# One core of Trainium2, a two-layer decoder trunk: the first mixer's transposes behind the gate's blocks, both halves' outputs together, the small inverses by one transfer

## The chip, the core and the metric

The kernel runs on one core of one Trainium2 chip. The metric is the device time of an execution in microseconds; the kernel before has a median of 2877.74 us over three runs (2874.36 to 2878.88). Engine names: PE is TensorE's matmul side and PEld its weight load, DVE is VectorE, ACT is ScalarE, POOL is GpSimd, SP is SyncE, which issues most of the DMAs.

## The reference, cut to what matters

Two layers of 2048 columns on 256 rows. Layer 0 is a gated DeltaNet, layer 1 a sparse attention; each is followed by a layer norm, a gated feed-forward block and a gated addition. Only layer 0's mixer is touched:

```python
def gdn_mixer(x, w_in, conv_w, a_log, dt_bias, norm_g, w_o):
    proj = x @ w_in                                   # q, k, v, z, a, b
    qkv = silu(causal_dwconv(qkv, conv_w))            # 4 taps
    ...                                               # 32 value heads, 16 key heads, width 128
    o = gated_delta_rule(q, k, v, g, beta)            # per head: a unit lower triangular solve
    o = o * rsqrt(mean(square(o), -1) + RMS_EPS) * norm_g * silu(z)
    return o.reshape(B, L, GDN_V_W) @ w_o
```

## The kernel before, in words

All products are of float32 values split into a rounded part `hi` (ACT, line 109) and the rest `lo` (DVE, line 110). Weights come in tiles of 128x1024 through the function `weights`: one DMA into `raw` on SP, `hi`, `lo`, three buffers each. `gemm_t_steps` makes products with the weights stationary (`mm_ps`: 8 matmuls of 512 columns with `hi`, line 128, then 8 of 256 columns with `lo`, line 132, per tile); `gemm_steps` makes them with the activations stationary (`b_ps`: per tile 8 matmuls with `hi`, lines 154 and 155, and 4 with `lo`, line 158). Twelve such `b_ps` matmuls are called a block here.

The mixer works on eight groups of four value heads (`gdn_groups`). The tokens stand in two halves a = 0, 1 of 128. Group g goes through these functions:

- `keys`: the projections of k and q, each followed by the convolution (`conv`: on DVE `pd`, three `ac`, on ACT a tanh, on DVE the last product).
- `decays`, `sums`, `blocks` (together `front`): decay factors, norms, and the triangular matrix `L` of each half and head. Its 32x32 diagonal blocks go to DRAM and back into `ld`.
- `substitute`: inverts the diagonal blocks, 62 small operations on POOL (groups 1 to 6) or on DVE (groups 0 and 7). Then four DMAs on POOL's queue write the result `xi` to `tt` in DRAM, and POOL multiplies both halves of `L` by a mask (line 521), which leaves what is below the diagonal blocks.
- `values`: the projection of v with its convolution, and eight transposes `v_ps` (line 547), four for each half, followed by copies on ACT.
- `zgate`: the projection of the gate z, eight blocks of `b_ps`.
- `inverses`: four DMAs on POOL's queue read `tt` into `pm`; `w_ps` = `L` times `pm`, copied into `W` by one ACT operation for each half (line 537).
- `solve`: for each half `pm` times the right side, then three steps `y <- y0 - W y` (`s_ps`, line 526; DVE, line 576); the last one is `u`.
- `outputs`: for each half the product `o_ps` (lines 587, 588), four squares with sums on ACT (`sqs`, line 591), on DVE the mean (`of`, line 592) and an inverse root of 12 operations, four products `ot` (line 598), four transposes `ot_ps` (line 602), and the copies into `oT`.

For one group in program order: `values` of g, `zgate` of g, `keys` of g + 1, `inverses` of g, `front` of g + 1, `substitute` of g + 1, `solve` of g, `outputs` of g. In the last group `ahead` stands in the place of `keys`: it starts the mixer's output projection `x @ w_o` on those rows of `oT` that are there, three steps of two column blocks. A scheduler turns the program into an order for each engine: it takes instructions as they become ready by its own costs, weights first (a priority in `weights`). `after` adds a dependency by hand, without a semaphore unless `sync` is set. PSUM has four banks for `mm_ps` and `b_ps`, two for the tag `bk` (`w_ps`, `s_ps`, `o_ps`, `ot_ps`) and two for the tag `sp`.

Of the kernel before, what the change touches and what calls it, by code (L numbers as in the profile page):

```python
# [27 lines left out]
W_AHEAD = 1000  # L28


C_IDENT, C_TRI, C_OFF, C_CMIN, C_CAUSAL, C_XINIT, C_ONES, C_QMIN = 0, 128, 256, 384, 512, 640, 896, 1024
N_CONST = 1152


def constants():

    c = np.zeros((P, N_CONST), np.float32)
    i, j = np.arange(P)[:, None], np.arange(P)[None, :]
    c[:, C_IDENT:C_IDENT + P] = i == j
    c[:, C_TRI:C_TRI + P] = i <= j  # L40
    c[:, C_OFF:C_OFF + P] = i // 32 > j // 32
# [12 lines left out]
    b = np.where(d < 16, d, np.minimum(large, 31))  # L54
    return c, (np.arange(32)[:, None] == b[None, :]).astype(np.float32)
# [9 lines left out]
class Trunk:  # L65
    def __init__(self, nc, tc, ctx, t):
        self.nc, self.tc, self.t = nc, tc, t
        pool = lambda **k: ctx.enter_context(tc.tile_pool(**k))

        self.const = pool(name="const", bufs=1)  # L70
        self.hl = pool(name="hl", bufs=3)
        self.xtp = pool(name="xtp", bufs=1)
        self.big = pool(name="big", bufs=1)
        self.cp = pool(name="cp", bufs=1, side="right")
        self.wp = pool(name="wp", bufs=3, side="right")
        self.mm = pool(name="mm", bufs=4, space=PSUM)
# [6 lines left out]
        self.offm = cst[:, C_OFF - P:C_OFF - P + P]  # L83
# [297 lines left out]
    def gdn_groups(self, pool, gk, cw, ng, oT, load, gates, ahead):  # L381
# [13 lines left out]
        h4 = range(4)  # L395
        five = lambda ap: ap.rearrange("p (j r) t -> p j r t", r=2)

        def conv(n0, out):

            def done(n, ps):  # L400
                pd = pads[n % 2]
                self.fold(pool, pd[:, 3:], ps)
                ac = pool.tile([P, S], F32, tag="ac", name="ac", bufs=2)
                w = cw[:, :, n0 + n]
                nc.scalar.activation(ac, pd[:, 3:], AF.Identity, scale=w[:, 3:4])
                for k in (2, 1, 0):
                    nc.vector.scalar_tensor_tensor(ac, pd[:, k:k + S], w[:, k:k + 1], ac, op0=ALU.mult, op1=ALU.add)  # L407
                o = out(n)
                nc.scalar.activation(o, ac, AF.Tanh, scale=0.5)
                self.mark = nc.vector.scalar_tensor_tensor(o, o, 1.0, ac, op0=ALU.add, op1=ALU.mult)  # L410
            return done

        def decays(s):
# [88 lines left out]
        def substitute(s, behind=None):  # L502


            L, ld = s["L"], s["ld"]
            eng = nc.gpsimd if behind is None else nc.vector
            xi = pool.tile([P, 8, 32], F32, tag="xi", name="xi", bufs=2)
            tmp = pool.tile([P, 8, 32], F32, tag="xt", name="xt", bufs=2)
# [6 lines left out]
                    self.after(ins, behind)  # L515
                eng.tensor_tensor(xi[:, :m, i + 1:], xi[:, :m, i + 1:], tmp[:, :m, :w], op=ALU.subtract)
            tt = s["tt"] = self.dr.tile([8, 4, 8, 4, 32], F32, tag="tt", name="tt")
            for e in range(4):
                nc.gpsimd.dma_start(out=tt[:, :, :, e].rearrange("q b c j -> (q b) c j"), in_=xi[32 * e:32 * e + 32])
            for a in range(2):  # L520
                nc.gpsimd.tensor_tensor(L[:, a], L[:, a], bcast(self.offm, 4, 1), op=ALU.mult)

        def mul(lhs, rhs, ps=None, first=True, last=True):
            ps = ps if ps is not None else self.sp.tile([P, 4, P], F32, tag="bk", name="s_ps")
            for h in h4:
                nc.tensor.matmul(ps[:, h], lhs[:, h], rhs[:, h], start=first, stop=last)  # L526
            return ps

        def inverses(s):

            for b in range(4):
                nc.gpsimd.dma_start(out=pm[32 * b:32 * b + 32, :, 32 * b:32 * b + 32],
                                    in_=s["tt"][:, b].rearrange("q c e j -> (c e) q j"))
            for a in range(2):
                ps = self.sp.tile([P, 4, 96], F32, tag="bk", name="w_ps")
                mul(s["L"][:, a], pm[:, 4 * a:4 * a + 4, 32:], ps)
                nc.scalar.activation(W[:, a, :, 32:], ps, AF.Copy)

        def values(s):
            g, sv = s["g"], s["sv"]  # L540
            v = pool.tile([P, 4, S], F32, tag="v", name="v")
            self.gemm_t(w_in, 4096 + 512 * g, 512, self.xT, conv(32 + 4 * g, lambda n: v[:, n]))
            vt = s["vt"] = pool.tile([P, 2, 4, P], F32, tag="vt", name="vt")
            for a in range(2):
# [6 lines left out]
        def zgate(s):  # L551
            zs = s["zs"] = pool.tile([P, 2, 512], F32, tag="zs", name="zs")

            def done(a, ps):
                nc.scalar.activation(zs[:, a], ps, AF.Tanh, scale=0.5)
                nc.vector.scalar_tensor_tensor(zs[:, a], zs[:, a], 1.0, ps, op0=ALU.add, op1=ALU.mult)  # L556

            self.gemm(w_in, 8192 + 512 * s["g"], 512, lambda k: self.xT[:, k], KT, done)

        def solve(s):  # L560
            vt = s["vt"]
            u = s["u"] = pool.tile([P, 2, 4, P], F32, tag="u", name="u")
            for a in range(2):
                rhs = vt[:, a]
                if a:
                    ps = mul(s["n21"], u[:, 0])
                    for h in h4:
                        nc.vector.scalar_tensor_tensor(rhs[:, h], ps[:, h], s["nc1"][:, h:h + 1], rhs[:, h],
                                                       op0=ALU.mult, op1=ALU.add)
                y0 = pool.tile([P, 4, P], F32, tag="y0", name="y0")  # L570
                nc.scalar.activation(y0, mul(pm[:, 4 * a:4 * a + 4], rhs), AF.Copy)
                y = y0
                for i in range(3):
                    ps = mul(W[:, a], y)
# [3 lines left out]
        def outputs(s):  # L578

            g, u = s["g"], s["u"]  # L580
            ss = pool.tile([P, 2, 2, 2], F32, tag="oss", name="oss", bufs=2)
            f = pool.tile([P, 2, 2, 2], F32, tag="of", name="of", bufs=2)
            for a in range(2):
                ps = self.sp.tile([P, 4, P], F32, tag="bk", name="o_ps")
                for h in h4:
# [9 lines left out]
                fa = self.rsqrt(pool, f[:, a].rearrange("p j r -> p (j r)"), 4)  # L595
                ot = pool.tile([P, 4, P], F32, tag="y", name="ot", bufs=2)
                for h in h4:
                    nc.vector.scalar_tensor_tensor(ot[:, h], ps[:, h], fa[:, h:h + 1], s["zs"][:, a, h * P:(h + 1) * P],
                                                   op0=ALU.mult, op1=ALU.mult)
                ps = self.sp.tile([P, 4, P], F32, tag="bk", name="ot_ps")  # L600
                for h in h4:
                    nc.tensor.transpose(ps[:, h], ot[:, h], self.ident)
                hi = oT[:, 4 * g:4 * g + 4, 0, a * P:(a + 1) * P]
                lo = oT[:, 4 * g:4 * g + 4, 1, a * P:(a + 1) * P]
                nc.scalar.activation(hi, ps, AF.Identity, scale=ng)
                nc.vector.scalar_tensor_tensor(lo, ps, ng, hi.bitcast(F32), op0=ALU.mult, op1=ALU.subtract)

        def front(s):
            decays(s)
            sums(s)  # L610
            blocks(s)

        n = keys(0)
        front(n)
        for g in range(8):
            s = n
            values(s)
            if not g:
                substitute(s, self.mark)
            zgate(s)  # L620
            if g < 7:
                n = keys(g + 1)
            else:
# [4 lines left out]
            if g < 6:  # L628
                substitute(n)
            solve(s)  # L630
            outputs(s)
            if g == 6:
                substitute(n, s["f"])


    BLOCKS = ((0, 512), (512, 512), (1024, 512), (1536, 512))
# [249 lines left out]
    def run(self, out):  # L886
# [1 line left out]
        begun = [self.project_steps(t["gdn_w_o"], lambda k: self.oT[:, k], 32, i) for i in range(2)]  # L888

        def ahead():  # L890
            for _ in range(3):
                for g in begun:
                    next(g)

# [51 lines left out]
```

## Time and profile before

| | |
|---|---|
| median of three runs | 2877.74 us (2874.36 to 2878.88) |
| the profiled execution | 2870.2 us, its span 2868.4 us |
| PE busy | 2816.9 us, 98% of the span |
| DVE, ACT, POOL busy | 1883.4 us (66%), 1401.6 us (49%), 311.8 us (11%) |
| mean granted clock | 0.995 |

The first mixer takes about the first 790 us of the span; its groups follow each other every 88 us or so. The span is the time from the first to the last instruction of the profiled execution; 1.8 us lie around it. Busy times of PE come from modelled ends of pipelined matmuls, so the profile shows a wait shorter than it is. A wait is written as "who waited <- who released it: us in total, times, longest".

### The profile page before, as it was taken

To read this page: it belongs to the slowest core of one execution; us is meant where nothing else is said; L and a number is where in the kernel's file an instruction comes from. 1 tells how busy PE (TensorE), PEld (TensorE's weight loads), DVE (VectorE), ACT (ScalarE), POOL (GpSimd) and SP (SyncE) were. 2 spreads that over 40 slices of the span, in tenths; PEclk is the share of its full clock that TensorE was granted. 3 is DMA by queue.
4 is the path that set the end of the run, shared out by engine and by line. 5 is a ranking of instruction groups with operands and counts; after the bars stand their busy time and mean duration, and the time that the engine had idled before them with its cause. 6 is when DMAs were issued, how large, how long until landed. Compare 5 with 4: busy or idle time off the path is not lost.

```text
span 2868.4 us, 40302 instructions
## 1 busy us (share of the span) xinstructions
PE 2816.9 (98%) x15022; PEld 2406.3 (84%) x15022; DVE 1883.4 (66%) x3256; ACT 1401.6 (49%) x2147; POOL 311.8 (11%) x580
## 2 busy tenths in 40 slices
PE   8999999999999999999999999999999999999999
PEld 6788888888787888888888888888888888888887
DVE  6878877778655666666554755766576666654565
ACT  4455555555334655555433544455365555543354
POOL 0143234540000000000000000210000000000000
PEclk9999999999999999999999999999999999999999
DMA  6655556655465566666656566554656666656555
GB/s 195 174 154 152 162 158 164 173 151 144 140 221 176 185 201 202 200 204 205 194 194 192 191 190 182 173 157 138 195 167 196 194 191 197 198 191 191 191 190 191
DMA packets 409620, 520.90 MB, mean 182 GB/s; under 512 B 28268, under 2 KB 296944, under 8 KB 409168
## 3 DMA queue, kind: packets, MB, share of 16 engines
q1 hardware_dynamic: 402192, 499.91, 57.4%
q0 software_dynamic: 7232, 18.42, 2.6%
q8 instruction: 118, 1.93, 0.3%
q14 instruction: 78, 0.64, 0.1%
HBM read 514.00 MB, written 7.39 MB: 182 GB/s over the span
## 4 chain that ended last, share of the span: by engine, by line
PE 90%; DVE 5%; ACT 2%; DMA 2%; issue 1%; POOL 0%; SPq 0%; ACTq 0%; DVEq 0%; POOLq 0%
PE mm_ps L128 32%; PE mm_ps L132 16%; PE b_ps L158 12%; PE b_ps L155 11%; PE b_ps L154 11%; PE s_ps L526 2%; DVE lo L110 1%; ACT sqs L591 1%; PE w_ps L526 1%; ACT hi L109 1%; DMA raw<-in_gdn_w_in 1%; PE n_ps L283 1%; DVE ac L407 1%; PE o_ps L588 0%; PE g_ps L479 0%
## 5 line engine op out<-in xcount | busy, mean ns | idle before, releaser
L110 DVE TENSOR_TENSOR lo<-raw,hi 128x1024 fp32r<-128x1024 f32 x925 | 1135.4, 1228 | 805.1 <-ACT hi L109 771.9
L109 ACT ACTIVATE hi<-raw 128x1024 fp32r<-128x1024 f32 x925 | 977.5, 1057 | 1227.7 <-PE b_ps L155 499.9
L128 PE MATMUL mm_ps<-xT,hi 128*128 128x512 f32 x4176 | 1068.1, 396 | 1.1 <-DVE xT L193 1.1
L128 PEld LDWEIGHTS mm_ps<-xT,hi 128*128 128x128 f32 x4176 | 752.8, 190 | 135.7 <-DVE xT L193 1.7
L132 PEld LDWEIGHTS mm_ps<-xT,lo 128*128 128x128 f32 x4176 | 575.3, 190 | 40.9
L132 PE MATMUL mm_ps<-xT,lo 128*128 128x256 f32 x4176 | 602.8, 284 | 0.0
L154 PE MATMUL b_ps<-hi,xT 128*128 128x512 f32 (+1 forms) x704 | 272.3, 389 | 0.4 <-DVE xT L292 0.4
L155 PE MATMUL b_ps<-hi,xT 128*128 128x512 f32 (+1 forms) x704 | 272.5, 389 | 0.0
L154 PE MATMUL b_ps<-hi,hTA 128*128 128x512 f32 x512 | 199.4, 390 | 0.0
L155 PE MATMUL b_ps<-hi,hTA 128*128 128x512 f32 x512 | 199.2, 389 | 0.0
L158 PE MATMUL b_ps<-lo,xT 128*128 128x512 f32 (+1 forms) x704 | 197.1, 392 | 0.0
L155 PEld LDWEIGHTS b_ps<-hi,xT 128*128 128x128 f32 x704 | 133.6, 190 | 25.4 <-issue 0.4
L154 PEld LDWEIGHTS b_ps<-hi,xT 128*128 128x128 f32 x704 | 132.8, 189 | 26.1 <-DVE xT L292 0.7
L158 PEld LDWEIGHTS b_ps<-lo,xT 128*128 128x128 f32 x704 | 130.2, 190 | 25.1
L158 PE MATMUL b_ps<-lo,hTA 128*128 128x512 f32 x512 | 136.9, 389 | 0.0
L205 POOL DMA_DIRECT2D lng<-in_ln_g x16 | 8.7, 546 | 1123.8 <-DVE lo L110 556.4
L158 PEld LDWEIGHTS b_ps<-lo,hTA 128*128 128x128 f32 x512 | 96.1, 188 | 20.0
L155 PEld LDWEIGHTS b_ps<-hi,hTA 128*128 128x128 f32 x512 | 96.1, 188 | 19.9
L154 PEld LDWEIGHTS b_ps<-hi,hTA 128*128 128x128 f32 x512 | 96.1, 188 | 19.9
L154 PE MATMUL b_ps<-hi,oT 128*128 128x512 f32 x256 | 100.4, 392 | 0.3 <-DVE zs L556 0.3
L155 PE MATMUL b_ps<-hi,oT 128*128 128x512 f32 x256 | 100.2, 391 | 0.0
L512 POOL TENSOR_TENSOR xt<-ld,xi 128x60 f32<-128x60 f32 (+24 forms) x186 | 86.0, 462 | 69.3 <-DMA ld<-lt 55.2
(261 smaller groups left out, 2585.7 us busy)
## 6 DMA issues: line engine op xcount, KB each, us to landing
raw<-in_gdn_w_in SPq DMA_DIRECT2D x193, 512.0 KB, 3.9
raw<-in_ffn_w_gate SPq DMA_DIRECT2D x160, 512.0 KB, 3.9
raw<-in_ffn_w_up SPq DMA_DIRECT2D x160, 512.0 KB, 3.6
raw<-in_ffn_w_down SPq DMA_DIRECT2D x160, 512.0 KB, 3.7
raw<-in_dsa_w_in SPq DMA_DIRECT2D x80, 512.0 KB, 3.6
raw<-in_gdn_w_o SPq DMA_DIRECT2D x64, 512.0 KB, 3.7
raw<-in_ple_w_gate SPq DMA_DIRECT2D x64, 512.0 KB, 4.1
raw<-in_dsa_w_o SPq DMA_DIRECT2D x32, 512.0 KB, 3.8
```

The costliest lines, as they stand in the source:

```text
L109: nc.scalar.activation(hi, raw, AF.Copy)
L110: ins = nc.vector.tensor_tensor(lo, raw, hi.bitcast(F32), op=ALU.subtract)
L128: nc.tensor.matmul(q[:m, :], hi[:, k, o:o + m], x[:, k0 + k].rearrange("p a b -> p (a b)"), start=k0 + k == 0, stop=False)
L132: nc.tensor.matmul(q[:m, S:], lo[:, k, o:o + m], x[:, k0 + k, 0, :], start=False, stop=k0 + k == kt - 1)
L154: nc.tensor.matmul(ps[a][:, :n], xh, hi[:, k, :], start=k0 + k == 0, stop=False)
L155: nc.tensor.matmul(ps[a][:, :n], xl, hi[:, k, :], start=False, stop=False)
L158: self.last = nc.tensor.matmul(ps[a][:, :n], x(k0 + k)[:, 0, a * P:(a + 1) * P], lo[:, k, :], start=False, stop=k0 + k == kt - 1)
L283: ins = nc.tensor.transpose(ps[:, k, a * P:(a + 1) * P], x[:, a, (k0 + k) * P:(k0 + k + 1) * P], self.ident)
L407: nc.vector.scalar_tensor_tensor(ac, pd[:, k:k + S], w[:, k:k + 1], ac, op0=ALU.mult, op1=ALU.add)
L512: ins = eng.tensor_tensor(tmp[:, :m, :w], bcast(ld[:, i + 1:, i], m, 1), xi[:, :m, i:i + 1].to_broadcast([P, m, w]), op=ALU.mult)
L526: nc.tensor.matmul(ps[:, h], lhs[:, h], rhs[:, h], start=first, stop=last)
L591: nc.scalar.activation(sq, ps[:, h], AF.Square, accum_out=ss[:, a, h // 2, h % 2:h % 2 + 1])
```

## The change

- `values` no longer issues its transposes; it hands back two functions, one for each half, and `zgate` calls one of the waiting functions after its 4th, 5th, 6th, ... block. Each makes four transposes.
- `outputs` computes `o_ps` and the squares of both halves first, then one inverse root for all eight heads, then the eight products `ot`. Its transposes are handed to the next group's `zgate` in the same way, ahead of that group's `v_ps`; the last group's are issued at the end. A dependency makes the first of four wait for the last of the products.
- In `solve` the second half's product with `pm` waits until all four heads of its right side are there.
- `substitute` writes `xi` by one DMA in the place of four. The mask is gone from the constants and from POOL: `L` stays as it is, and `inverses` copies only the blocks below the diagonal into `W`, by three ACT operations for each half on 32, 64 and 96 partitions.
- Group 0's substitution may start behind the second of the four heads' convolution in the place of the last (`marks[-3]`).
- `ahead` makes five steps of each of its two column blocks in the place of three.

```diff
-            for e in range(4):
-                nc.gpsimd.dma_start(out=tt[:, :, :, e].rearrange("q b c j -> (q b) c j"), in_=xi[32 * e:32 * e + 32])
-            for a in range(2):
-                nc.gpsimd.tensor_tensor(L[:, a], L[:, a], bcast(self.offm, 4, 1), op=ALU.mult)
+            nc.gpsimd.dma_start(out=tt.rearrange("q b c e j -> e (q b) c j"), in_=xi)
...
-                nc.scalar.activation(W[:, a, :, 32:], ps, AF.Copy)
+                for b in (1, 2, 3):
+                    nc.scalar.activation(W[:32 * b, a, :, 32 * b:32 * b + 32], ps[:32 * b, :, 32 * b - 32:32 * b], AF.Copy)
...
-            self.gemm(w_in, 8192 + 512 * s["g"], 512, lambda k: self.xT[:, k], KT, done)
+            for j, _ in enumerate(self.gemm_steps(w_in, 8192 + 512 * s["g"], 512, lambda k: self.xT[:, k], KT, done)):
+                if j > 2 and rest:
+                    rest.pop(0)()
...
-                nc.scalar.activation(y0, mul(pm[:, 4 * a:4 * a + 4], rhs), AF.Copy)
+                nc.scalar.activation(y0, mul(pm[:, 4 * a:4 * a + 4], rhs, start=ins if a else None), AF.Copy)
...
+            fa = self.rsqrt(pool, f.rearrange("p a j r -> p (a j r)"), 8)
+
+            def gate(a):
                 ot = pool.tile([P, 4, P], F32, tag="y", name="ot", bufs=2)
                 for h in h4:
-                    nc.vector.scalar_tensor_tensor(ot[:, h], ps[:, h], fa[:, h:h + 1], s["zs"][:, a, h * P:(h + 1) * P],
-                                                   op0=ALU.mult, op1=ALU.mult)
+                    ins = nc.vector.scalar_tensor_tensor(ot[:, h], parts[a][:, h], fa[:, 4 * a + h:4 * a + h + 1],
+                                                         s["zs"][:, a, h * P:(h + 1) * P], op0=ALU.mult, op1=ALU.mult)
+
+                def turn():
...
+                        t = nc.tensor.transpose(ps[:, h], ot[:, h], self.ident)
+                        if not h:
+                            self.after(t, ins, sync=True)
...
-            values(s)
+            rest += values(s)
             if not g:
-                substitute(s, self.mark)
-            zgate(s)
+                substitute(s, self.marks[-3])
+            zgate(s, rest)
...
-            outputs(s)
+            rest = outputs(s)
...
-            for _ in range(3):
+            for _ in range(5):
                 for g in begun:
                     next(g)
```

The order of the work on PE at the end of group 4's solve, before (`s_ps` is the last product of the solve, `o_ps<-u,qd` the output of the first half, `v_ps` two heads of the next group's values, four transposes):

```order
L128 MATMUL mm_ps<-xT,hi 128x512
L526 MATMUL s_ps<-y,W 128x128 x4
L588 MATMUL o_ps<-u,qd 128x128 x4
L128 MATMUL mm_ps<-xT,hi 128x512 x7
L132 MATMUL mm_ps<-xT,lo 128x256 x8
L547 MATMUL v_ps<-ident,v 128x128 x4
```

and of the change at the same place (`o_ps<-u,qo` opens each head of the second half):

```order
L126 MATMUL mm_ps<-xT,hi 128x512 x2
L522 MATMUL s_ps<-y,W 128x128 x4
L595 MATMUL o_ps<-u,qd 128x128 x4
L594 MATMUL o_ps<-u,qo 128x128
L595 MATMUL o_ps<-u,qd 128x128
```

The second half's output, which stood in the gate's second block, now follows the first half's at once, and the transposes of `v` are gone from ahead of the gate's first block.

The gate's blocks of the next group on PE, before, in the second block:

```order
L602 MATMUL ot_ps<-ident,ot 128x128
L155 MATMUL b_ps<-hi,xT 128x512
L154 MATMUL b_ps<-hi,xT 128x512
L155 MATMUL b_ps<-hi,xT 128x512
L158 MATMUL b_ps<-lo,xT 128x512 x3
L602 MATMUL ot_ps<-ident,ot 128x128
L158 MATMUL b_ps<-lo,xT 128x512
L602 MATMUL ot_ps<-ident,ot 128x128 x2
L587 MATMUL o_ps<-u,qo 128x128
```

and of the change, behind the fourth block:

```order
L153 MATMUL b_ps<-hi,xT 128x512
L156 MATMUL b_ps<-lo,xT 128x512 x4
L614 MATMUL ot_ps<-ident,ot 128x128 x4
L152 MATMUL b_ps<-hi,xT 128x512
L153 MATMUL b_ps<-hi,xT 128x512
```

Four transposes of `ot` stand behind the 4th and behind the 5th block; `v_ps` stand in the same way behind the 6th and the 7th.

PE in group 0, before, from the first sums (`ss_ps`) to the first `w_ps`:

```order
L455 MATMUL ss_ps<-cst,sq 128x1 x4
L479 MATMUL g_ps<-k 128x256 x2
L128 MATMUL mm_ps<-xT,hi 128x512 x2
L132 MATMUL mm_ps<-xT,lo 128x256 x8
L128 MATMUL mm_ps<-xT,hi 128x512 x8
L132 MATMUL mm_ps<-xT,lo 128x256 x8
L128 MATMUL mm_ps<-xT,hi 128x512 x5
L526 MATMUL w_ps<-pm,L 128x96 x8
```

and of the change:

```order
L126 MATMUL mm_ps<-xT,hi 128x512 x6
L453 MATMUL ss_ps<-cst,sq 128x1 x4
L477 MATMUL g_ps<-k 128x256 x2
L522 MATMUL w_ps<-pm,L 128x96 x8
L522 MATMUL s_ps<-vt,pm 128x128 x4
```

In group 0 `w_ps` moves ahead of 15 matmuls with `hi` and 16 with `lo`. In group 7 it stands behind ten blocks of the output projection, where it stood behind six and a half.

## Rows read from the trace of the kernel before

**Rows 1.** The page, busy time by engine.

```profile
PE 2816.9 (98%) x15022; PEld 2406.3 (84%) x15022; DVE 1883.4 (66%) x3256; ACT 1401.6 (49%) x2147; POOL 311.8 (11%) x580
```

**Rows 2.** Windows: one group's stretch; PE, PEld, DVE, ACT, POOL busy, PEclk, DMA, GB/s.

```profile
512.00:600.00 88.00, 87.04 (x515) 75.56 (x515) 69.18 (x160) 47.55 (x92) 37.50 (x74) 1.00 0.59 162
```

**Rows 3.** Waits of PE from 80 to 790 us: us in total, times, longest.

```profile
PE ot_ps L602 <- DVE ot L598: 8.0, 14, 2.0
PE w_ps L526 <- DMA pm<-tt: 6.2, 2, 3.9
PE v_ps L547 <- DVE v L410: 4.6, 9, 1.3
```

**Rows 4.** Timeline of PE, 515 to 542 us: start, us, line, operation, [idle before <- releaser].

```profile
517.83 1.06 PE L588 MATMUL o_ps<-u,qd 128*128 128x128 f32 x8
...
520.34 1.11 PE L132 MATMUL mm_ps<-xT,lo 128*128 128x256 f32 x8
521.30 0.60 PE L547 MATMUL v_ps<-ident,v 128*128 128x128 f32 x4
...
521.97 0.39 PE L155 MATMUL b_ps<-hi,xT 128*128 128x512 f32 x1
...
523.58 1.07 PE L158 MATMUL b_ps<-lo,xT 128*128 128x512 f32 x4
524.49 0.39 PE L154 MATMUL b_ps<-hi,xT 128*128 128x512 f32 x1
...
533.11 0.44 PE L547 MATMUL v_ps<-ident,v 128*128 128x128 f32 x2 [0.31 <-DVE v L410]
...
537.11 0.27 PE L602 MATMUL ot_ps<-ident,ot 128*128 128x128 f32 x1
...
537.45 0.27 PE L602 MATMUL ot_ps<-ident,ot 128*128 128x128 f32 x1
```

**Rows 5.** Timeline of DVE, 515 to 530 us.

```profile
518.15 0.68 DVE L576 TENSOR_TENSOR u<-y,s_ps 128x512 f32<-128x512 f32 x1
...
520.68 0.16 DVE L592 SCALAR_TENSOR_TENSOR of<-oss,wq 128x4 f32<-128x4 f32 x1 [0.23 <-ACT sqs L591]
...
521.99 1.26 DVE L110 TENSOR_TENSOR lo<-raw,hi 128x1024 fp32r<-128x1024 f32 x1
...
525.74 0.34 DVE L598 SCALAR_TENSOR_TENSOR ot<-o_ps,rs,zs 128x128 f32<-128x128 f32 x1
```

**Rows 6.** Groups of instructions on ACT, 80 to 790 us: busy, mean ns, idle before.

```profile
L591 ACT ACTIVATE sqs<-o_ps 128x128 f32<-128x128 f32 x64 | 17.7, 276 | 25.3 <-PE o_ps L588 23.9
...
L537 ACT ACTIVATE W<-w_ps 128x384 f32<-128x384 f32 x16 | 7.8, 491 | 12.3 <-PE w_ps L526 12.3
```

**Rows 7.** Waits of PE from 700 to 800 us (group 7).

```profile
PE w_ps L526 <- DMA pm<-tt: 3.9, 1, 3.9
PE ot_ps L602 <- DVE ot L598: 2.8, 3, 2.0
```

**Rows 8.** Waits of PE from 80 to 160 us (group 0).

```profile
PE v_ps L547 <- DVE v L410: 2.4, 2, 1.3
PE w_ps L526 <- DMA pm<-tt: 2.2, 1, 2.2
PE ss_ps L455 <- ACT sq L452: 0.4, 1, 0.4
```

**Rows 9.** Windows: the stretch behind group 7's wait; PEclk third from the right.

```profile
748.40:751.80 3.40, 3.40 (x19) 3.40 (x18) 0.00 (x0) 0.98 (x2) 0.00 (x0) 0.51 0.02 6
```

**Rows 10.** Chain that ended last, 700 to 800 us (group 7): start, us, what.

```profile
747.98 3.30 PE w_ps L526 x16
```

**Rows 11.** Chain that ended last, 80 to 160 us (group 0).

```profile
126.69 1.71 POOL tt L519 x3
128.40 3.48 DMA tt<-xi
...
138.21 2.00 PE w_ps L526 x16
```

More of the change, by code (lines that the diff above doesn't have):

```diff
@@ L28 @@
 W_AHEAD = 1000
-C_IDENT, C_TRI, C_OFF, C_CMIN, C_CAUSAL, C_XINIT, C_ONES, C_QMIN = 0, 128, 256, 384, 512, 640, 896, 1024
-N_CONST = 1152
+C_IDENT, C_TRI, C_QMIN, C_CMIN, C_CAUSAL, C_XINIT, C_ONES = 0, 128, 256, 384, 512, 640, 896
+N_CONST = 1024
 def constants():
@@ L82, in __init__ @@
         self.tri = cst[:, C_TRI - P:C_TRI - P + P]
-        self.offm = cst[:, C_OFF - P:C_OFF - P + P]
         self.cmin = cst[:, C_CMIN - P:C_CMIN - P + P]
@@ L394, in gdn_groups @@
             nc.gpsimd.memset(pd[:, 0:3], 0.0)
-        h4 = range(4)
+        h4, self.marks = range(4), []
         five = lambda ap: ap.rearrange("p (j r) t -> p j r t", r=2)
@@ L409, in done @@
                 nc.scalar.activation(o, ac, AF.Tanh, scale=0.5)
-                self.mark = nc.vector.scalar_tensor_tensor(o, o, 1.0, ac, op0=ALU.add, op1=ALU.mult)
+                self.marks.append(nc.vector.scalar_tensor_tensor(o, o, 1.0, ac, op0=ALU.add, op1=ALU.mult))
             return done
@@ L502, in substitute @@
         def substitute(s, behind=None):
-            L, ld = s["L"], s["ld"]
+            ld = s["ld"]
             eng = nc.gpsimd if behind is None else nc.vector
@@ L517, in substitute, with mul @@
             tt = s["tt"] = self.dr.tile([8, 4, 8, 4, 32], F32, tag="tt", name="tt")
-            for e in range(4):
-                nc.gpsimd.dma_start(out=tt[:, :, :, e].rearrange("q b c j -> (q b) c j"), in_=xi[32 * e:32 * e + 32])
-            for a in range(2):
-                nc.gpsimd.tensor_tensor(L[:, a], L[:, a], bcast(self.offm, 4, 1), op=ALU.mult)
-        def mul(lhs, rhs, ps=None, first=True, last=True):
+            nc.gpsimd.dma_start(out=tt.rearrange("q b c e j -> e (q b) c j"), in_=xi)
+        def mul(lhs, rhs, ps=None, start=None):
             ps = ps if ps is not None else self.sp.tile([P, 4, P], F32, tag="bk", name="s_ps")
             for h in h4:
-                nc.tensor.matmul(ps[:, h], lhs[:, h], rhs[:, h], start=first, stop=last)
+                ins = nc.tensor.matmul(ps[:, h], lhs[:, h], rhs[:, h], start=True, stop=True)
+                if start is not None and not h:
+                    self.after(ins, start, sync=True)
             return ps
@@ L543, in values, with turn @@
             vt = s["vt"] = pool.tile([P, 2, 4, P], F32, tag="vt", name="vt")
-            for a in range(2):
+            def turn(a):
                 ps = self.sp.tile([P, 4, P], F32, tag="sp", name="v_ps")
@@ L549, in values, with zgate @@
                     nc.scalar.activation(vt[:, a, h], ps[:, h], AF.Identity, scale=sv[:, a, h // 2, h % 2:h % 2 + 1])
-        def zgate(s):
+            return [lambda: turn(0), lambda: turn(1)]
+        def zgate(s, rest):
             zs = s["zs"] = pool.tile([P, 2, 512], F32, tag="zs", name="zs")
@@ L567, in solve @@
                     for h in h4:
-                        nc.vector.scalar_tensor_tensor(rhs[:, h], ps[:, h], s["nc1"][:, h:h + 1], rhs[:, h],
-                                                       op0=ALU.mult, op1=ALU.add)
+                        ins = nc.vector.scalar_tensor_tensor(rhs[:, h], ps[:, h], s["nc1"][:, h:h + 1], rhs[:, h],
+                                                             op0=ALU.mult, op1=ALU.add)
                 y0 = pool.tile([P, 4, P], F32, tag="y0", name="y0")
-                nc.scalar.activation(y0, mul(pm[:, 4 * a:4 * a + 4], rhs), AF.Copy)
+                nc.scalar.activation(y0, mul(pm[:, 4 * a:4 * a + 4], rhs, start=ins if a else None), AF.Copy)
                 y = y0
@@ L582, in outputs @@
             f = pool.tile([P, 2, 2, 2], F32, tag="of", name="of", bufs=2)
+            parts = []
             for a in range(2):
@@ L594, in outputs @@
                 s.setdefault("f", ins)
-                fa = self.rsqrt(pool, f[:, a].rearrange("p j r -> p (j r)"), 4)
+                parts.append(ps)
+            fa = self.rsqrt(pool, f.rearrange("p a j r -> p (a j r)"), 8)
+            def gate(a):
                 ot = pool.tile([P, 4, P], F32, tag="y", name="ot", bufs=2)
                 for h in h4:
-                    nc.vector.scalar_tensor_tensor(ot[:, h], ps[:, h], fa[:, h:h + 1], s["zs"][:, a, h * P:(h + 1) * P],
-                                                   op0=ALU.mult, op1=ALU.mult)
[L600 to L606, printed above, removed]
+                    ins = nc.vector.scalar_tensor_tensor(ot[:, h], parts[a][:, h], fa[:, 4 * a + h:4 * a + h + 1],
+                                                         s["zs"][:, a, h * P:(h + 1) * P], op0=ALU.mult, op1=ALU.mult)
+                def turn():
+                    ps = self.sp.tile([P, 4, P], F32, tag="bk", name="ot_ps")
+                    for h in h4:
+                        t = nc.tensor.transpose(ps[:, h], ot[:, h], self.ident)
+                        if not h:
+                            self.after(t, ins, sync=True)
+                    hi = oT[:, 4 * g:4 * g + 4, 0, a * P:(a + 1) * P]
+                    lo = oT[:, 4 * g:4 * g + 4, 1, a * P:(a + 1) * P]
+                    nc.scalar.activation(hi, ps, AF.Identity, scale=ng)
+                    nc.vector.scalar_tensor_tensor(lo, ps, ng, hi.bitcast(F32), op0=ALU.mult, op1=ALU.subtract)
+                return turn
+            return [gate(a) for a in range(2)]
         def front(s):
@@ L611, in front @@
             blocks(s)
-        n = keys(0)
+        n, rest = keys(0), []
         front(n)
@@ L630, in gdn_groups @@
             solve(s)
-            outputs(s)
+            rest = outputs(s)
             if g == 6:
                 substitute(n, s["f"])
+        for turn in rest:
+            turn()
     BLOCKS = ((0, 512), (512, 512), (1024, 512), (1536, 512))
```

1 line of the change is left out of this document (removed).

## The prediction

> **What bounds the kernel now.** I read the page's busy times first: PE is busy for 2816.9 of 2868.4 us [rows 1]. So a change that gives PE neither more nor less work can gain at most the 51 us in which PE stands still, plus what the profile hides of each wait. Next the windows, to see where PE stands still: a middle group has 87.04 us of PE in 88.00 [rows 2], so most of what is there to gain lies in small pieces. Then the waits of PE over the mixer [rows 3]: the reader is to see three kinds, transposes of outputs that wait for their products (8.0 us, 14 times), transposes of values that wait for the convolution (4.6 us, 9 times), and two waits of `w_ps` for the DMA into `pm` (6.2 us). The change aims at these three and at no other.
>
> These numbers are too small, and the timeline of PE says by how much [rows 4]. Four `b_ps` matmuls start from 523.58 to 524.49 us, 0.227 us apart, but one of them is shown for 0.39 us. So each wait behind such a matmul hides 0.16 us more. 14 x 0.16 = 2.2 and 9 x 0.16 = 1.4 us: the waits are 10.3 us for `ot_ps`, 6.1 us for `v_ps`, 6.5 us for `w_ps`.
>
> **Four in a row.** Is it worth something in itself? From 521.30 to 521.97 us lie four transposes and one `b_ps` matmul [rows 4]: 0.67 - 0.23 = 0.44, 0.11 us for a transpose. From 537.11 to 537.45 us lie one transpose and one `b_ps` matmul between two transposes: 0.34 - 0.23 = 0.11 us. A single one costs no more than one of four, so grouping is worth nothing, and only the waits count. The same holds for the second half's products with `pm`.
>
> **Transposes of outputs.** They move from the second and fourth block to behind the fourth and fifth. PE gets there 4 x 12 x 0.227 = 10.9 us after the gate began, and to the second four 0.44 + 2.7 us later. When are they ready? Now the first product `ot` starts at 525.74 us [rows 5], 4.4 us after the end of the values' projection (521.30 us). The change delays it: DVE's `of` waits for four more squares, 276 ns each [rows 6]; with the reading of the sum I allow 0.5 us each, 2.0 us. So the first product starts 6.4 us after the gate's start. On DVE one `lo` (1.26 us) stands ahead of the fourth product and a second one ahead of the eighth; with 0.34 us for a product [rows 5] four are there after 6.4 + 4 x 0.34 + 1.26 = 9.0 us, eight after 11.6 us. PE needs four at 10.9 and eight at 14.1 us. So these waits go, but for group 7: there no gate follows, 32 `b_ps` matmuls (7.3 us) stand between output and transposes, and the work is longer than before by the four squares and a second `lo`. I leave its waits of 0.8 + 2 x 0.16 = 1.1 us as they are (the 2.8 us of [rows 7] less the 2.0 of group 6). Gain 10.3 - 1.1 = **9.2 us**.
>
> **Transposes of values.** They come behind the sixth and seventh block, 10.9 + 2 x (0.44 + 2.72) = 17.2 us after the gate's start. The last `v` of a group is now waited for in the third block, at 533.11 us [rows 4], 11.8 us after the gate's start. The change puts four more products and the wait for the squares ahead of it: 11.8 + 4 x 0.34 + 2.0 = 15.2 us. So they go in groups 1 to 7: 6.1 less group 0's 2.4 + 2 x 0.16 = 2.7 [rows 8], a gain of **3.4 us**.
>
> **The last inverse.** Group 7's `w_ps` waits 3.9 + 0.16 = 4.1 us for `pm` [rows 7]. Behind it the granted clock is 0.51, that is 1.2 GHz in the place of 2.4 GHz [rows 9]: the 16 matmuls take 3.30 us [rows 10], against 2.00 us in group 0 [rows 11]; with the products behind them I put the loss at 1.6 us. The change lets 120 in the place of 79 `b_ps` matmuls stand ahead, 41 x 0.227 = 9.3 us, and takes three of the four transfers' issue off the chain, 1.7 us [rows 11]. 9.3 is over twice 4.1, so wait and slow clock both go: **5.7 us**.
>
> **Group 0.** Its waits are 2.7 us for `v_ps` and 2.2 + 0.16 = 2.4 us for `w_ps` [rows 8], 5.1 in all. I don't count on them. The order puts `w_ps` ahead of 15 matmuls with `hi` and 16 with `lo`: 15 x 0.227 + 16 x 0.12 = 5.3 us (eight with `lo` take 520.34 to 521.30 us [rows 4]), while the transfer brings `pm` 1.7 us earlier, and what the substitution's earlier start brings no row shows. What was waited for at the transposes is waited for at the sums of squares (`ss_ps`, which already waits 0.4 us) and at `w_ps`. The gain lies between 0 and 5.1; I take **0.5 us**, nearer to the lower end since DVE, the engine waited for, has no less to do there.
>
> **What it costs.** The second half's `o_ps` follows the solve without cover: `u` runs from 518.15 to 518.83 us while the first half's `o_ps` runs from 517.83 us for 8 x 0.11 = 0.9 us [rows 4, 5]; PE can go on with the first pair of the second half for 0.2 us. That just covers it; I charge 0.1 us in seven groups, rounded to **0.5 us** lost. The copies into `W` become three for each half: the row is 491 ns for 384 columns and 276 ns for 128 [rows 6], so 0.83 us in the place of 0.49, hidden behind the product with `pm` (0.9 us) and other matmuls. The mask on POOL and three issues of a DMA in each group leave the path to `pm`, which in groups 1 to 6 nobody waits for: nothing. DVE saves 12 small operations in each group, which shows in no wait of PE: nothing. The one bigger transfer instead of four small ones carries the same bytes in the same pieces: nothing beyond the 1.7 us counted.
>
> **The sum.** 9.2 + 3.4 + 5.7 + 0.5 - 0.5 = 18.3 us. The profiled execution took 2870.2 us, so it would take 2851.9 us. It stands 7.5 us below the median of the runs, 2877.74 us; from the median I forecast **2859 us**. A measurement of this kernel tells about 0.2%, 5.8 us, from no change.
>
> **A rule against it.** After 3.9 us without work PE went to half its clock; after the 2.2 us in group 0 it did not [rows 7, 8, 9]. The Trainium skill, TensorE: Matmul & The Clock Gate, Part 1, says that the array's clock is gated by how busy the engine has been, and that idleness sends it back to half. By that rule a longer wait at group 0's early `w_ps` would cost as much as in group 7, and the sum would be 16.7 us in the place of 18.3.
>
> **The rivals.** *The waits come back in part.* PE, freed of one wait, arrives earlier at the next thing that DVE makes. For it: group 0 looks just so. Against it: in a middle group only 1 us of 88 is idle [rows 2], and DVE is idle for 19 of them. If half of the 12.6 us for `ot_ps` and `v_ps` comes back, the gain is 12 us: 2866 us.
>
> *Group 0's waits go too*, because DVE's earlier start brings `pm` in time: 4.6 us more, 2854 us.
>
> *The transposes wait in full at their new places*, so that the change does not do what it says: 18.3 - 12.6 = 5.7 us, only the last inverse: 2872 us. Against it stand the margins of 1.9 to 2.5 us above.
>
> *Slower: DVE's queue is blocked.* DVE now waits for eight squares at `of`, and the `lo` of the gate's second block stands behind it, now at 521.99 to 523.25 us [rows 5]. PE wants it 8 x 0.227 us into the block that starts at 524.49 us [rows 4], at 526.3 us: 3 us of slack. The price is what the wait exceeds 3 us by, in eight groups. To eat up 18.3 us and 5.8 more, it has to be 6 us, against 2.0 us for four squares: 2884 us or more. The Trainium skill, TensorE: Matmul & The Clock Gate, Architectural detail, says that ACT and DVE take their queues strictly in order, so nothing behind `of` could pass it; the trace agrees, since DVE stood idle for 0.23 us ahead of that `of`, with the `lo` behind it [rows 5].
>
> **How the numbers follow.** The forecast 0.60, waits back in part 0.17, group 0 too 0.10, the transposes wait in full 0.08, slower 0.05. Range 2850 to 2870 us: it takes in the forecast, group 0's gain and the half that comes back, and at the lower end a run that is like the profiled one. Faster by over 0.2%: 0.60 + 0.17 + 0.10 = 0.87; within: 0.08; slower: 0.05.
>
> **What would show it.** Right: no wait `ot_ps <- DVE ot` but about 1 us in group 7; no `v_ps <- DVE v` from group 1 on; no `w_ps` wait and no half clock near 750 us; PE's busy time unchanged within 2 us. In group 0 a wait of 2 to 4 us at `w_ps` near 130 us. Wrong: new waits of `b_ps` for `lo`, or of `o_ps` for `u` by more than 0.3 us each; or the wait of `w_ps` in group 0 gone.

## The result, and the profile after

The changed kernel takes 2896.8 us (median of 6 runs, 2881.8 to 2900.4) beside 2873.5 us for the kernel before (median of 6 as well): a ratio of 1.0075, interval 1.0057 to 1.0093. It is slower by about 0.75%, where the forecast was 2859 us, a gain. The profiled execution took 2900.35 us at a mean granted clock of 0.986 (before: 2870.2 us, 0.995).

Busy times of the changed kernel, from its page; they answer to [rows 1]:

```profile
span 2898.5 us, 40122 instructions
...
PE 2830.6 (98%) x15022; PEld 2425.1 (84%) x15022; DVE 1872.5 (65%) x3160; ACT 1403.9 (48%) x2179; POOL 287.5 (10%) x540
```

PE does the same 15022 matmuls, but is shown busy for 13.7 us more: a part of them ran at half clock. The waits of PE in the mixer, 80 to 790 us, answer to [rows 3] (us in total, times, longest):

```profile
PE w_ps L522 <- DMA pm<-tt: 27.3, 7, 7.7
PE v_ps L548 <- DVE v L408: 5.8, 1, 5.8
PE b_ps L152 <- DVE zs L560: 0.6, 1, 0.6
```

All waits of `ot_ps` are gone, and all of `v_ps` but one, as forecast (group 7's outputs come later than 790 us here; one wait of 0.2 us stands there). In their place stand seven waits of `w_ps` for `pm`, where there were two: every group but the last waits. Group 5 in three views. First POOL (start, us, what, idle before and who ended it):

```profile
580.68 0.22 POOL L514 TENSOR_TENSOR xi<-xi,xt 128x8 f32<-128x8 f32 x1
581.22 2.07 POOL L516 DMA_DIRECT2D tt<-xi  x1 [0.32 <-POOL xi L514]
593.91 2.31 POOL L530 DMA_DIRECT2D pm<-tt  x4 [10.62 <-DMA tt<-xi]
```

Then PE, and the windows (PE, PEld, DVE, ACT and POOL busy, with counts; granted clock; DMA share; GB/s), where the first one answers to [rows 2]:

```profile
600.21 3.70 PE L522 MATMUL w_ps<-pm,L 128*128 128x96 f32 x16 [4.33 <-DMA pm<-tt]
```

```profile
512.00:600.00 88.00, 83.89 (x485) 73.13 (x483) 65.48 (x140) 45.41 (x86) 33.54 (x68) 0.98 0.57 155
600.00:606.00 6.00, 5.79 (x26) 5.73 (x27) 1.52 (x5) 1.96 (x8) 0.00 (x0) 0.50 0.29 88
```

From the issue of the one transfer into `tt` to the first transfer into `pm` lie 12.7 us. The same place of the kernel before, in its group 4:

```profile
469.65 2.32 POOL L519 DMA_DIRECT2D tt<-xi  x4 [0.30 <-POOL xi L516]
475.97 2.32 POOL L532 DMA_DIRECT2D pm<-tt  x4 [3.99 <-DMA tt<-xi]
```

There it is 6.3 us. Over all eight groups this handover takes 9.6 to 12.7 us in the changed kernel and 5.8 to 6.7 us before. The one transfer is issued in 2.07 us where four took 2.32, but lands much later. That is why `w_ps` waits 4.3 us, and behind the wait the clock is 0.50, so that the 16 matmuls take 3.70 us where [rows 11] has 2.00. The landing times, each counted from a transfer's own issue, before and then after:

```profile
L519 POOL DMA_DIRECT2D tt<-xi x32: 576/601/633, 126.7 to 737.5; - x32
...
DMA to landing us min/median/max: 2.1/3.7/4.4
```

```profile
L516 POOL DMA_DIRECT2D tt<-xi x8: 2040/2070/2125, 127.5 to 773.9; - x8
...
DMA to landing us min/median/max: 9.0/10.5/12.1
```

One more reading of the kernel before shows why this costs anything at all. The last transfer into `pm` in group 3 (the only one in the window 390.4 to 390.8 us) and the `w_ps` that needs it:

```profile
L532 POOL DMA_DIRECT2D pm<-tt x1: 584/584/584, 390.3 to 390.3; - x1
...
DMA to landing us min/median/max: 5.0/5.0/5.0
```

```profile
395.45 0.74 PE L526 MATMUL w_ps<-pm,L 128*128 128x96 f32 x5
```

It landed at 395.3 us, and `w_ps` began at 395.45. No wait is shown, yet the slack was under 0.2 us. This is the tightest group: the same subtraction gives 0.4 and 0.7 us in groups 4 and 5, and 4.2, 4.4 and 3.1 us in groups 1, 2 and 6.

### The profile page after: what moved, and what is told of

It is laid out like the page before. It is cut to its first block, busy times and chain, and to the rows that moved or that the text cites. A ratio compares the mean times of both kernels' runs of the same rounds, so it can differ in the third digit from the quotient of the medians.

```text
span 2898.5 us, 40122 instructions
## 1 busy us (share of the span) xinstructions
PE 2830.6 (98%) x15022; PEld 2425.1 (84%) x15022; DVE 1872.5 (65%) x3160; ACT 1403.9 (48%) x2179; POOL 287.5 (10%) x540
## 4 chain that ended last, share of the span: by engine, by line
PE 68%; DVE 1%; ACT 1%; issue 1%; DMA 0%; ACTq 0%
PE mm_ps L126 25%; PE mm_ps L130 13%; PE b_ps L156 10%; PE b_ps L153 10%; PE b_ps L152 10%; PE n_ps L281 0%; PE sc_ps L833 0%; PE lg_ps L883 0%; ACT hi L107 0%; DVE lo L108 0%; DMA raw<-in_ple_w_gate 0%; ACT xb L287 0%; PE po_ps L899 0%; ACT x L271 0%; DVE st L226 0%
## 5 line engine op out<-in xcount | busy, mean ns | idle before, releaser
L156 PE MATMUL b_ps<-lo,xT 128*128 128x512 f32 (+1 forms) x704 | 190.8, 387 | 0.0
```

The source lines that it names most:

```text
L156: self.last = nc.tensor.matmul(ps[a][:, :n], x(k0 + k)[:, 0, a * P:(a + 1) * P], lo[:, k, :], start=False, stop=k0 + k == kt - 1)
```

## The experiments

**Four transfers again.** In the changed kernel, only this:

```diff
-            nc.gpsimd.dma_start(out=tt.rearrange("q b c e j -> e (q b) c j"), in_=xi)
+            for e in range(4): nc.gpsimd.dma_start(out=tt[:, :, :, e].rearrange("q b c j -> (q b) c j"), in_=xi[32 * e:32 * e + 32])
```

> The changed kernel with the four transfers of before in the place of the one (nothing else is undone; the mask stays away). Theory A, the loop: from the end of one group's w_ps over L, the small DMAs, POOL's substitution, tt and pm to the next w_ps the trace of before shows 85 us, with w_ps itself 87 us, as long as PE's own work in a group. So the one transfer's 4 to 5 us more are what made the changed kernel slower, and with four the w_ps waits of groups 1 to 6 shrink from 2.5 to 5 us to about 1 us each, but do not vanish, because PE, freed of its transposes, now arrives earlier: about 2863 us (2858 to 2868). Theory B, only the transfer is to blame and PE has slack: no w_ps wait at all in groups 1 to 6, about 2855 us, my forecast's sum. Theory C, something else slows the changed kernel: 2890 us or more.

Measured: 2852.4 us, ratio to before 0.9941 (0.9925 to 0.9958). Its waits of PE from 80 to 790 us, all of them:

```profile
PE v_ps L548 <- DVE v L408: 5.2, 1, 5.2
PE w_ps L522 <- DMA pm<-tt: 2.4, 1, 2.4
PE b_ps L152 <- DVE zs L560: 0.6, 1, 0.6
PE ot_ps L614 <- DVE ot L608: 0.2, 1, 0.2
```

No `w_ps` waits in groups 1 to 6, and the time is that of theory B: the whole loss hangs on this line, 44 us by the medians and 38 by the two ratios. That PE has slack, as theory B says, it does not show: in groups 3 and 4 of this run `pm` landed 0.14 and 0.16 us ahead of `w_ps`.

**The one transfer in the kernel before**, the same line the other way round and nothing else.

> The kernel before with the one transfer in the place of four, and nothing else. Theory A (the loop fills a group): the handover from tt to pm takes 10 to 12 us in the place of 6, w_ps waits 2 to 5 us in each of groups 1 to 6, and the half clock behind each wait costs 1 to 1.5 us more: 2873 + 20 to 35 = 2893 to 2908 us. Theory B (slack of 2 us or more in a group): w_ps waits about 2 us in each, 2885 us. Theory C (the transfer is not to blame): within 5 us of before.

Measured: 2895.6 us (2886.6 to 2919.6, a wide spread), ratio 1.0103 (1.0068 to 1.0139). Its first waits of PE from 80 to 790 us:

```profile
PE w_ps L526 <- DMA pm<-tt: 19.4, 5, 7.7
PE ot_ps L602 <- DVE ot L598: 6.3, 13, 0.8
PE v_ps L547 <- DVE v L410: 5.5, 8, 2.1
```

This is about as slow as the changed kernel, though all the old waits of the transposes are there: the intervals of the two ratios overlap. Of the 19.4 us, 7.7 lie in group 0 and 7.2 in group 7. In groups 1 to 6 `w_ps` waits 4.5 us, and 1.1 more that the view puts down to "issue", where the changed kernel has 19.6. With the late landing no gain of the moved transposes is left to be seen: the time saved in one place is waited for at the next `w_ps`.

**Two transfers** of 64 partitions, in the changed kernel:

```diff
-            nc.gpsimd.dma_start(out=tt.rearrange("q b c e j -> e (q b) c j"), in_=xi)
+            for e in (0, 2): nc.gpsimd.dma_start(out=tt[:, :, :, e:e + 2].rearrange("q b c e j -> e (q b) c j"), in_=xi[32 * e:32 * e + 64])
```

> The changed kernel with two transfers of 64 partitions each. If what makes the one slow is the size of its pieces (4096 bytes where four transfers have 2048), the handover from the first issue to pm lies between, about 8 us: 2875 us. If only the number of issues counts, it is no longer than with four, 6 us or 5.5: like the run with four, 2855 to 2863 us. If any transfer over more than 32 partitions is slow, like the one: 2890 us or more.

Measured: 2938.6 us, ratio 1.0235 (1.0219 to 1.025). The last expectation comes nearest, but "like the one" foresaw nothing worse than one transfer. Each transfer has half the bytes, takes as long to issue and lands later:

```profile
L516 POOL DMA_DIRECT2D tt<-xi x16: 2041/2301/2548, 126.3 to 809.0; - x16
...
DMA to landing us min/median/max: 10.2/12.1/14.4
```

The median of the first of the two is 11.6 us, of the second, issued behind it, 13.4. So neither bytes nor the number of issues set the landing. What is left is the pattern, and the next two kernels ask which part of it.

**One transfer, adjacent bytes; one transfer, 128-byte pieces in three dimensions.** Both in the changed kernel:

```diff
+            nc.gpsimd.dma_start(out=tt.rearrange("q b c e j -> (q b c e j)").rearrange("(p c j) -> p c j", p=128, c=8), in_=xi)
```

```diff
-            tt = s["tt"] = self.dr.tile([8, 4, 8, 4, 32], F32, tag="tt", name="tt")
+            tt = s["tt"] = self.dr.tile([8, 4, 8, 4, 64], F32, tag="tt", name="tt")
+            nc.gpsimd.dma_start(out=tt.rearrange("q b c e j -> (q b c e) j").rearrange("(p c) j -> p c j", c=8)[:, :, :32], in_=xi)
```

> The changed kernel with its one transfer, but into 1024 adjacent bytes for each of the 128 partitions (tt is written in another order and read as before, so the inverses are wrong and the outputs with them; the work is the same). If the pattern of the destination makes the one transfer slow (four dimensions, 128-byte pieces), the handover from tt to pm shrinks from 10 to 12 us to 6 us or less, and the time is that of the run with four transfers, 2852 us or a little under. If it is the 128 partitions or the 128 KB, it stays at 2890 us or more.

> The changed kernel with its one transfer, into 128-byte pieces that lie 256 bytes apart, in a pattern of three dimensions (tt is twice as large and, as in the run before, written in another order; the work is the same, the inverses are wrong). If the small pieces make the one transfer slow: handover 10 us or more and about 2895 us. If it is the fourth dimension: 6 us and about 2852 us.

Measured: 2857.1 us (0.9949, 0.9934 to 0.9963) and 2856.8 us (0.9948, 0.9931 to 0.9964). Their transfers, adjacent bytes first:

```profile
L516 POOL DMA_DIRECT2D tt<-xi x8: 568/622/622, 126.4 to 729.6; - x8
...
DMA to landing us min/median/max: 2.3/3.7/4.7
```

```profile
L516 POOL DMA_DIRECT2D tt<-xi x8: 868/875/921, 126.4 to 736.0; - x8
...
DMA to landing us min/median/max: 3.7/4.3/5.1
```

All 128 partitions, all 128 KB, and in the second kernel the small pieces too, land in 4 us. Two things are left that only the late transfers have. Their destination's outermost dimension is small: 4 (`e`) in the one transfer, 2 in each of the two, against 32 in the four and 128 in these kernels. And their destination has four dimensions, where those that land in 4 us have three or fewer. No run has four dimensions with a large outermost one, so the times alone don't part the two. Landing follows the outermost dimension: 12.1 us at 2, 10.5 at 4, 3.7 to 4.3 at 32 and 128. A shorter handover than that of the four transfers gains nothing: no faster than 2852 us.

The traces' packet records say more. In every group `tt` is written in 32 packets of 4096 bytes by the one transfer, by the two, and by each of these two kernels. Of the one transfer's at most 5 or 6 are under way at the same time, of both halves' together 4 or 5, and of these two kernels' 7 to 17. So the late transfers move few packets at a time, as few as their outermost dimension or little more. (They also make 96 and 224 packets of 128 bytes more in each group; what those cost no run shows.)

The Trainium skill, DMA: Bandwidth & Descriptors, Rules for kernel authors, states a rule that would give this: a transfer is spread over as many DMA engines as its slowest dimension allows, and an outermost dimension smaller than 16 keeps it on at most so many. The order of the landings and the packets under way agree. The profile doesn't name the engine of a packet, so that engines are what limits them is the page's.

**Is the loop as long as PE's work?** Two kernels move the landing by a little. On POOL behind the substitution of groups 1 to 6 in the run with four transfers:

```diff
+            if behind is None: [nc.gpsimd.tensor_copy(xi, xi) for _ in range(2)]
```

> As the run with four transfers, with two copies of xi onto itself on POOL between the substitution and the transfers of groups 1 to 6, about 2.2 us. Theory, the group's loop and PE's work are of the same length with four transfers, so each microsecond on the loop shows: the trace of that run has pm landing 0.1 to 0.2 us ahead of w_ps in groups 3 and 4, but 4 to 5 us ahead in groups 1, 2, 5 and 6. If the loop holds in every group: 6 x 2.2 = 13 us more, 2866 us. If only the two groups without slack pay: 4 us more, 2857 us. If PE has slack that the landing does not show: no change.

Measured: 2857.0 us, ratio 0.9951 (0.9932 to 0.997). The copies are shorter than I had put them, 0.4 us each by their median, and the waits of `w_ps` rise from one of 2.4 us to three:

```profile
PE w_ps L523 <- DMA pm<-tt: 4.9, 3, 2.1
```

The two new ones are 1.3 us in group 1 and 1.5 us in group 3, one of them in a group with 4 to 5 us of slack in the run without copies. That is more than 0.8 us of copies can use up: the slack moves from run to run. The kernels below that have four transfers and no copies show it too, three of them with one wait of 0.9 to 1.5 us in a group from 3 to 5. So these waits can't be put down to the copies, and the 4.6 us in the medians are within the intervals: what a microsecond on the loop costs is not shown by this kernel.

And the kernel before with the one transfer into adjacent bytes, the line shown above:

> The kernel before with one transfer into adjacent bytes (tt in another order, the inverses are wrong, the work is the same). The loop is 1 to 2 us shorter than with four transfers. If before was held by PE and not by the loop in groups 1 to 6, only the waits of w_ps in groups 0 and 7 shrink (2.4 and 4.1 us, and the half clock behind the second): 2871 - 3 to 7 = 2864 to 2868 us. If the loop held before too: 2855 us, the order's gain without the order.

Measured: 2869.0 us, ratio 0.9986 (0.9976 to 0.9995). As expected for a kernel held by PE in groups 1 to 6: about 4 us, and the transposes still wait 7.4 and 5.4 us. In groups 1 to 6 `pm` now lands 4.4 to 7.7 us ahead of `w_ps`, and the groups take the same 88 us: slack was made, and no group got shorter.

The firmest reading of the loop is the time from one group's `w_ps` to the next one's. For group 5, `w_ps` of groups 4 and 5 in the kernel before, then with four transfers, then group 4's in the changed kernel (group 5's there is shown above, at 600.21 us):

```profile
483.15 1.92 PE L526 MATMUL w_ps<-pm,L 128*128 128x96 f32 x16
570.79 1.92 PE L526 MATMUL w_ps<-pm,L 128*128 128x96 f32 x16
```

```profile
477.60 1.98 PE L522 MATMUL w_ps<-pm,L 128*128 128x96 f32 x16
563.71 1.92 PE L522 MATMUL w_ps<-pm,L 128*128 128x96 f32 x16
```

```profile
506.35 2.34 PE L522 MATMUL w_ps<-pm,L 128*128 128x96 f32 x16 [2.33 <-DMA pm<-tt]
```

That is 87.6, 86.1 and 93.9 us. The same for groups 2 to 6, beside the handover from the first issue of `tt` to that of `pm`, in us:

| | from `w_ps` to `w_ps` | handover | the first less the second |
|---|---|---|---|
| before | 87.6 to 88.2 | 6.3 to 6.7 | 81.1 to 81.5 |
| four transfers | 86.0 to 86.2 | 5.3 to 6.1 | 80.0 to 80.8 |
| changed kernel | 89.5 to 95.9 | 9.6 to 12.7 | 79.9 to 83.6 |
| two transfers | 96.9 to 100.1 | 14.3 to 16.6 | 81.1 to 84.3 |

In the last two, where `w_ps` waits in each of these groups, a group takes what its handover takes and 80 to 84 us more. With a handover of 6 us such a loop is 86 to 90 us long, which is as long as PE's own work in a group.

**The last inverse**, in the kernel before and then in the run with four transfers, the number of steps ahead:

```diff
-            for _ in range(3):
+            for _ in range(5):
```

> The kernel before with five steps ahead in the last group and nothing else, the part of the change that my forecast priced at 5.7 us: 2872 - 5.7 = 2866 us, with no wait of w_ps and no half clock near 750 us. What the run with four transfers (2852 us) is faster than this is then the moved transposes' share, 12 to 13 us by the forecast. Rival: the two steps ahead only move the same blocks, and the wait comes back at the transposes of the last outputs: 2870 us or more.

> As the run with four transfers, but with three steps ahead in the last group as before. Both theories: group 7's w_ps waits about 4 us again and runs at half clock behind it, 5 us more than with five steps. Rival: the chain of group 7 is shorter by the mask and by DVE's earlier start, so that the wait is under 1 us: no difference that can be measured.

Measured: before with five steps 2865.6 us, 0.9985 (0.9975 to 0.9996), 4 us less; four transfers with three steps 2860.2 us, 0.9961 (0.9946 to 0.9976), 8 us more than with five by the medians and 6 by the ratios, whose intervals overlap; there group 7's `w_ps` waits 4.3 us where [rows 7] has 3.9, and group 4's 1.3 us. From 735 to 755 us the first shows no half clock:

```profile
735.00:755.00 20.00, 20.00 (x102) 16.95 (x101) 8.69 (x8) 8.40 (x9) 4.65 (x8) 1.00 0.69 212
```

From this kernel to the run with four transfers it is 0.9985 - 0.9941 = 0.0044, or 12.6 us, give or take some 6 by the two intervals: the moved transposes with the rest.

**The mask.** Four transfers, and the mask on POOL with one copy into `W` for each half, as before:

```diff
+            for a in range(2):
+                nc.gpsimd.tensor_tensor(s["L"][:, a], s["L"][:, a], bcast(self.offm, 4, 1), op=ALU.mult)
...
-                for b in (1, 2, 3):
-                    nc.scalar.activation(W[:32 * b, a, :, 32 * b:32 * b + 32], ps[:32 * b, :, 32 * b - 32:32 * b], AF.Copy)
+                nc.scalar.activation(W[:, a, :, 32:], ps, AF.Copy)
```

> As the run with four transfers, with the mask on POOL and the single copy into W for each half as before. My forecast charged and credited the mask with nothing in groups 1 to 6: within 3 us of 2852 us. Rival: POOL's 2.5 us for the mask lie on the chain to pm, which has little slack: w_ps waits again, 2860 us or more.

Measured: 2856.5 us, 0.995 (0.9935 to 0.9965). The 4 us lie within the intervals; `w_ps` waits once for 2.3 us, in group 0, so the rival falls. Yet the trace shows a price: in groups 2 to 6 it is 86.5 to 86.7 us from `w_ps` to `w_ps`, half a microsecond more than with four transfers alone, and `s_ps` waits for `y` seven times, 1.8 us in all. Whether the mask or the single copy makes it was not tried.

**Group 0.** Two kernels with four transfers: its substitution behind the last convolution again, and its transposes of values two blocks later.

```diff
-                substitute(s, self.marks[-3])
+                substitute(s, self.marks[-1])
```

```diff
-                if j > 2 and rest:
+                if j > (2 if s["g"] else 4) and rest:
```

> As the run with four transfers, but group 0's substitution again starts behind the last of the four heads' convolution, as before. In the run with four, DVE's queue stood for 5.1 us at the first operation of that substitution, which waited for ld, with the convolution of the values behind it, and PE waited 5.2 us at v_ps and ran at half clock. Theory: that wait falls to 2 to 3 us, the half clock goes, and tt is issued no later (126.7 us before, 127.0 us with four): 2 to 4 us faster, about 2849 us. Rival: the substitution ends later by as much and the wait moves to w_ps: the same time, 2852 us.

> As the run with four transfers, but group 0's transposes of values come two blocks later (in group 0 nothing of an earlier group is in the way). In that group PE waits 5.2 us at v_ps behind DVE, which stands at its first operation of the substitution for ld, with the convolution and the next lo behind it. If PE has work there that doesn't need DVE, the wait shrinks by up to 5.4 us: 2847 us. If the next block's lo stands in the same queue, PE waits there in its place: the same, 2852 us.

Measured: 2853.2 us (0.994, 0.9924 to 0.9957) and 2853.0 us (0.9937, 0.9925 to 0.995), both as with four transfers alone. What DVE waits for from 86 to about 100 us, in the run with four transfers and then with the substitution behind the last convolution:

```profile
DVE xt L510 <- DMA ld<-lt: 5.1, 1, 5.1
```

```profile
DVE lo L108 <- ACT hi L107: 6.0, 1, 6.0
```

In the first, DVE stands at the substitution for `ld`. Let that go behind the convolution, and DVE stands for a `hi` instead; PE waits 5.8 us at `v_ps`. With later transposes PE waits 5.2 us in two pieces. Both expectations of a gain fell. Whether DMA traffic holds `ld` and the weights back there was not tried.

The run with four transfers beats both kernels, 2852.4 us; none of its variants is faster.

## Why the prediction was wrong

Wrong sign, by one term. Point by point:

- **Transposes of outputs** (9.2 us): right. Their waits are 8.0 us in [rows 3] and none from 80 to 790 us in the changed kernel. I had left 1.1 us for group 7; 0.2 us are there, in the changed kernel and with four transfers.
- **Transposes of values** (3.4 us): right in groups 1 to 7, where no wait is left. The two terms together are 12.6 us, 1.6 us for each group; by the table above a middle group takes 1.7 us less with four transfers than before.
- **The last inverse** (5.7 us): right as far as the noise tells; 4 to 8 us in the two runs that change it alone. One part of it was wrong: I took 1.7 us off the chain for three issues fewer, and the one issue takes 2.07 us where four took 2.32, so 0.25 us are saved.
- **What it costs** (0.5 us for `o_ps`, nothing for three copies, POOL's mask and DVE): no wait of `o_ps` or for `W` appears. DVE's `of` waits 15.8 us for the squares in the place of 6.9, 13 times in both traces, and no wait of PE comes of it.
- **Group 0** (0.5 us gained): wrong, but small. With four transfers `v_ps` waits 5.2 us and `w_ps` 2.4, against 2.4 and 2.2 in [rows 8], and at the first wait the clock falls:

```profile
96.00:100.00 4.00, 3.34 (x10) 2.75 (x11) 3.10 (x8) 0.95 (x2) 0.00 (x0) 0.50 0.49 132
```

- **The step that failed**: "The one bigger transfer instead of four small ones carries the same bytes in the same pieces: nothing beyond the 1.7 us counted." I priced a transfer by its bytes and its issue. It lands 10.5 us after its issue where each of the four lands after 3.7, the handover to `pm` is about 5 us longer, and by the run with four transfers that costs 44 us (38 by the ratios).
- **The step beside it**: the path to `pm`, "which in groups 1 to 6 nobody waits for: nothing". That PE doesn't wait says nothing of slack. From one `w_ps` over `L`, `ld`, POOL's substitution, `tt` and `pm` to the next `w_ps` is a loop, and the kernel before ran it in 88 us with under 0.2 us to spare in group 3. Once it is longer than PE's own work, each group takes the loop's time, as the table above has it. DVE carries the delay on:

```profile
DVE L L424 <- PE w_ps L522: 23.0, 7, 9.9
```

In the changed kernel DVE starts the next group's `L` that much later, so the lateness is not made up in the next group. The size in the profiled runs: `w_ps` waits 27.3 us against 2.4 with four transfers, 25 us. The mean clock is 0.986 over 2898.5 us against 0.996 over 2846.1, which is 81 and 23 us at half clock, so up to 29 us lost by slow matmuls; a part of the half clock lies in the waits and is counted twice. Together at most 54, where the two executions, 2900.35 and 2847.91 us, differ by 52.

Behind 5.2 us at `v_ps` (four transfers) and 4.3 us at `w_ps` (changed kernel, group 5) the clock was 0.50, the lower of its two levels. By the rule that I weighed (the Trainium skill, TensorE: Matmul & The Clock Gate, Part 1) this was to be expected, and these two stretches agree; but I had looked for it in group 0 alone, and the waits came in every group from 0 to 6. The length of a wait alone doesn't tell whether the clock falls: behind 2.50 us in group 2 it stayed at 1.00, and behind 2.33 us in group 4 it was 0.50 from 508.7 us on:

```profile
325.00:331.00 6.00, 6.00 (x43) 5.65 (x44) 4.97 (x13) 2.54 (x10) 0.00 (x0) 1.00 0.46 136
508.70:514.70 6.00, 6.00 (x23) 5.45 (x23) 4.20 (x13) 1.79 (x6) 0.00 (x0) 0.50 0.13 45
```

None of the rivals was what happened. The slower one (DVE blocked at `of`) showed no wait of PE for `lo`, and the half that "comes back in part" had the right idea, a freed PE that arrives early at the next thing, without the loop that makes it all come back. Of the sum without the one transfer, 18.3 us, the run with four transfers shows 2871.2 - 2852.4 = 18.8, with an interval of 12 to 22. That it comes so close is in part luck: group 0's term and the 1.7 us were wrong. As printed, two steps of the working are also 0.1 us off (8.0 + 2.2 and 4.6 + 1.4), which changes nothing.

## What to carry to other kernels

Price a merged transfer by its access pattern, its outermost dimension first (the number of dimensions was not parted from it here), and not by bytes or issues: look for a transfer of the same pattern in the trace, and where none is there, give its landing a range. Ahead of lengthening a path that nobody waits for, subtract the landing from the start of its user in every group; where the difference is near zero and the path runs through a loop from group to group, what exceeds it is paid in each round. And try the parts of a change one by one: here one line hid some 18 us of gain.

## What the runs showed of the hardware

I had not expected that cutting a transfer in two makes each half land later (11.6 and 13.4 us for 64 KB each, 10.5 us for 128 KB), nor that the issue on POOL's queue takes by pattern 0.62 to 2.3 us for the same partitions or fewer. The gaps ahead of `w_ps`, 3.9 us on average (27.3 / 7), cost by the estimate above up to as much again through the granted clock.
